# A two-layer encoder trunk: the input also laid out with features as rows, per-feature vectors as columns

## The chip, the core and the metric

The kernel runs on one core of a Trainium2 chip. The metric is the device time of one execution in microseconds, taken as the median of several runs; smaller is better. The engines are TensorE (PE in the profile; its weight loads are shown apart as PEld), VectorE (DVE), ScalarE (ACT), GpSimd (POOL) and SyncE (SP, which here only issues DMA loads and stores).

## The reference

The input `x` has 512 tokens of 1024 features, in float32. The first layer normalises each token (RMSNorm with a gain per feature, `a_norm_g`), multiplies by one wide input matrix, and splits the result into latents for attention, channels for pooling, and a gate. The second layer is a retention layer, and a last RMSNorm follows. The part that the change touches is the start of the first layer:

```python
def rms_norm(x, g):
    xf = x.astype(jnp.float32)
    y = xf * lax.rsqrt(jnp.mean(xf * xf, axis=-1, keepdims=True) + NORM_EPS)
    return (y * g.astype(jnp.float32)).astype(x.dtype)

def hybrid_attn_pool_layer(x, cos_a, sin_a, norm_g, w_in, ...):
    h = rms_norm(x, norm_g)
    proj = h @ w_in
    cq, ckv, kr, u, gate = jnp.split(proj, list(EVEN_SPLITS), axis=-1)
    ...
    y = jnp.concatenate([a, b], axis=-1) * jax.nn.silu(gate)
    return y @ w_out

x = x + hybrid_attn_pool_layer(x, ...)
```

`cq` (the query latents) are the first 384 columns of `proj`, `ckv` (the key and value latents) the next 128, `kr` the next 64. The per-feature vectors besides `a_norm_g` are the gains of the two latent norms, the scale of the pooling channels, the gain of the second layer's norm and the gain of its group norm: 3, 1, 8, 8 and 16 rows of 128.

## The kernel before

**Layout.** Features lie on the 128 partitions and the 512 tokens along the free dimension, so that `proj` comes out turned, 128 outputs by 512 tokens at a time. TensorE sums over the partitions, hence both the weights and the activations must have features on partitions. The weights lie so in memory; `x` lies with tokens as rows, and the kernel turns it on TensorE with an identity matrix (L264), 128 by 128 at a time, into PSUM.

**Precision.** Every product of two matrices is made of three (`mm3`, L71 to L76). Each operand is split into a high part, the value rounded to TensorE's fast float32 form, and a low part, what is left. ScalarE writes the high part (a copy, L108, L281), VectorE subtracts it for the low part (L109, L282). The products are high by high (L72), high weights by low activations (L75), and low weights by high activations (L76).

**The norm.** The gain per feature is applied before the product, as a scale per partition (L275 and L276, with the column `cols0`). The factor per token, called R, is applied behind it: squares of `x` by rows on ScalarE (L338, which adds up along the features), a sum (L340), the power of minus one half on GpSimd (L177), and a broadcast over all partitions on TensorE (`bcast`, L194 to L214: two products with a matrix of ones, L212 and L213), copied to SBUF by L343. `keep_R` (L332) multiplies a finished product by R while it empties the product's PSUM bank.

**The first stage.** `x_pair(q)` prepares two feature tiles: eight transpositions, the split of `x` times gain, the split of the weights of the 384 query latents, and a copy of the turned `x` to SBUF (L285, L286), which is later the residual. Four such pairs feed three outputs of 128 that are held in three PSUM banks (`held`), 72 products in all. Behind them comes the turn of the 36 per-feature rows into columns (L315), then R, then the 24 products of the key and value latents (`gemm_T`, L347), then 16 products for `kr` (L359, L360), then pooling and gates. Of PSUM's eight banks four have the name mm, two tr, two sc. With three held and one for the key and value latents, the bank for `kr` comes free when `keep_R` has run once.

**What sets the order.** The loads are issued by SP, in its program order, each landing at its own time; the weights go through four buffers (raw), split into four (wH) and three (wL). The first vector goes on ScalarE's queue. The framework's planner orders each engine's instructions beforehand: the earliest in program text that it reckons to be ready goes next. An instruction that is pinned (`keep_in_program_order`) is placed behind everything that was traced before it on its engine; what is traced after it may still be put ahead of it. The broadcast's first product (L212) and the instructions of `x_pair` on ScalarE and VectorE are pinned so. Six products with zeros (L160) run before the first load has landed.

Of the kernel before, what the change touches and what calls it, by code (L numbers as in the profile page):

```python
# [19 lines left out]
P = 128  # L20
# [12 lines left out]
QN, KVN, PSC, RN, GN = 0, 3, 4, 12, 20  # L33
NVEC = 36
# [3 lines left out]
def trunk(ctx: ExitStack, tc: tile.TileContext, x, positions, a_norm_g, a_w_in, a_q_norm_g, a_w_uq,  # L38
          a_kv_norm_g, a_w_ukv, a_pool_w, a_pool_scale, a_w_out, r_norm_g, r_w_in, r_decay_fwd,
          r_decay_bwd, r_gn_g, r_w_out, final_norm_g, freqs, edges, out):  # L40
# [9 lines left out]
    def S(tag, shape=(P, T), dt=F32):  # L50
        count[0] += 1
        return sb.tile(list(shape), dt, tag=tag, name=f"{tag}_{count[0]}", bufs=BUFS[tag])

    def C(name, shape, dt=F32):
        return sb.tile(list(shape), dt, tag=name, name=name, bufs=1)
# [61 lines left out]
    cols0 = C("cols0", (P, 8))  # L117
    cols = C("cols", (P, 40))[:, 0:NVEC]
# [11 lines left out]
    vrow0 = S("t")[:8, :P]  # L130
    nc.scalar.dma_start(vrow0, a_norm_g.rearrange("o (k p) -> (o k) p", p=P))

    pin(nc.scalar.copy(fsum[:, 0:4], mhalf))
    xt = [[None] * 4 for _ in range(4)]

    def load_x(q):
        for i in range(2):
            v = S("l1").rearrange("p (t n) -> p t n", t=2)
            nc.sync.dma_start(v, x[0, i * 256:(i + 1) * 256, q * 256:(q + 1) * 256]
                              .rearrange("(t p) n -> p t n", p=P))  # L140
            xt[2 * i][q] = v[:, 0]
            xt[2 * i + 1][q] = v[:, 1]
# [6 lines left out]
    def load_pair(q):  # L149
        load_x(q)  # L150
        raws.append(wload(w_in[q * 256:(q + 1) * 256, 0:384].rearrange("(k p) n -> p k n", p=P), 2, 384))
# [7 lines left out]
    for i in range(6):  # L159
        mm(warm, lhsT=zero[:, 0:P], rhs=zero, start=True, stop=True)  # L160
# [4 lines left out]
    vps = PS("tr")  # L165
    nc.tensor.transpose(vps[:, :8], vrow0, ident[:8, :8])
    pin(V.tensor_copy(cols0, vps[:, :8]))

# [87 lines left out]
    hH, hL, xT = [], [], []  # L256
    held = [PS("mm") for _ in range(3)]

    def x_pair(q):
        pts = []  # L260
        for k in (2 * q, 2 * q + 1):
            pt = PS(("tr", "tr", "sc", "sc")[k % 4])
            for t in range(4):
                i = nc.tensor.transpose(pt[:, t * P:(t + 1) * P], xt[t][q][:, (k % 2) * P:(k % 2 + 1) * P], ident)  # L264
                if q == 1:
                    pin(i)
            pts.append(pt)
        raw, n = raws[q][:2]
        wh = S("wH", (P, 1024), F32R)
        wl = S("wL", (P, 1024), F32R)  # L270
        for i in range(2):
            k = 2 * q + i
            h = S("hT", dt=F32R)
            l = S("hT", dt=F32R)
            pin(act(h, pts[i], AF.Copy, scale=cols0[:, k:k + 1]))  # L275
            pin(V.scalar_tensor_tensor(out=l, in0=pts[i], scalar=cols0[:, k:k + 1], in1=f(h), op0=ALU.mult,  # L276
                                       op1=ALU.subtract))
            hH.append(h)
            hL.append(l)
            c = slice(i * n // 2, (i + 1) * n // 2)  # L280
            pin(nc.scalar.copy(wh[:, c], raw[:, c]))  # L281
            pin(V.tensor_sub(wl[:, c], raw[:, c], f(wh[:, c])))  # L282
        u = [w[:, :n].rearrange("p (k n) -> p k n", k=2) for w in (wh, wl)]
        xT.extend([S("xT"), S("xT")])
        pin(nc.scalar.copy(xT[-2], pts[0]))  # L285
        pin(V.tensor_copy(xT[-1], pts[1]))  # L286
        return u
# [6 lines left out]
    nc.sync.dma_start(posi, positions[0].partition_broadcast(P))  # L294
    for q in range(4):
        if 0 < q < 3:
            us.append(x_pair(q + 1))
        uH, uL = us[q]
        for k in (2 * q, 2 * q + 1):
            if k == 1:  # L300
                us.append(x_pair(1))
            for m in range(3):
                ms = slice(m * P, (m + 1) * P)
                mm3(held[m], uH[:, k % 2, ms], uL[:, k % 2, ms], hH[k], hL[k], k == 0, k == 7)

    pin(V.tensor_copy(posf, posi))
    vrow = S("t")[:NVEC, :P]
    for src, at, n in ((a_q_norm_g, QN, 3), (a_kv_norm_g, KVN, 1),
                       (a_pool_scale, PSC, 8), (r_norm_g, RN, 8), (r_gn_g, GN, 16)):
        nc.sync.dma_start(vrow[at:at + n, :], src.rearrange("o (k p) -> (o k) p", p=P))  # L310
# [3 lines left out]
    vps = PS("tr")  # L314
    nc.tensor.transpose(vps[:, :NVEC], vrow, ident[:NVEC, :NVEC])  # L315
    V.tensor_copy(cols, vps[:, :NVEC])

    def gemm_T(w, c0, nm, evac, hH, hL):

        for m in range(nm):  # L320
            uH, uL = w_cols(w, c0 + m * P)
            pt = PS("mm")
            for k in range(8):
                mm3(pt, uH[:, k], uL[:, k], hH[k], hL[k], k == 0, k == 7)
            evac(m, pt)
            tick(2)
# [8 lines left out]
    for q in range(4):  # L335
        for t in range(4):
            junk = S("t")
            act(junk[:, 0:256], xt[t][q], AF.Square, accum_out=ssq[:, 4 * t + q:4 * t + q + 1])  # L338
    ss = S("sm", (P, 4))
    V.tensor_reduce(out=ss, in_=ssq.rearrange("p (t q) -> p t q", q=4), axis=AX.X, op=ALU.add)  # L340
# [6 lines left out]
    gemm_T(w_in, 384, 1, keep_R, hH, hL)  # L347
# [715 lines left out]
```

## Time and profile before

| what | value |
|---|---|
| median of 3 runs | 794.64 us (794.26 to 794.81) |
| the profiled execution's own time | 794.41 us |
| its span, first to last instruction | 792.6 us |
| TensorE busy | 781.1 us, 99% |
| VectorE busy | 579.0 us, 73% |
| ScalarE busy | 403.4 us, 51% |
| moved by DMA | 80.91 MB, 102 GB/s on average |

The profile's times are microseconds from the start of the span. In a timeline each row gives the start, the duration, the engine, the line of the kernel, the operation, what is written and read, and how many instructions were merged into the row; in brackets stands the idle time of the engine before it and what ended it. TensorE's products overlap, so the distance between two starts tells their pace and the duration does not. A row of waits gives the engine and what it did, what it waited for, the sum, the number of times and the longest. A row of a stretch of time gives the stretch, its length, the busy time of each engine with its count of instructions, the granted clock of TensorE, the share of DMA and GB/s.

### The profile page before, as it was taken

Reading aid. Unit: us, or ns where it says so; the run is one execution under the profiler, and the core shown is the slowest. Engines: PE = TensorE matmul, PEld = TensorE weight load, DVE = VectorE, ACT = ScalarE, POOL = GpSimd, SP = SyncE. Lnnn points to the kernel's source line nnn. Section 1 sums busy time; section 2 is a strip of 40 time slices with the busy share of each in tenths; the row PEclk is TensorE's granted clock in tenths of the full one; section 3 lists DMA queues with packets and bytes.
Section 4 is the critical chain, followed back from the end, with each engine's and each line's share of the span. In section 5 each row is a group of like instructions: output and inputs, shape, how many; then the busy total and the mean of one; then the engine's idle time right before and its main releaser. Section 6 shows DMA issues by size and latency. Waiting matters only on the chain. (4 is left out here: it accounts for less than half of the span.)

```text
span 792.6 us, 9592 instructions
## 1 busy us (share of the span) xinstructions
PE 781.1 (99%) x3546; PEld 642.0 (81%) x3546; DVE 579.0 (73%) x938; ACT 403.4 (51%) x670; POOL 38.6 (5%) x60
## 2 busy tenths in 40 slices
PE   9999999999999999999999999999999999999996
PEld 7888888888888888888877888888888888888885
DVE  4689986768748677899679747787377884767845
ACT  6645346666626744318654832358333583334832
POOL 0010000000000000100010100100101001010003
PEclk9999999999999999999999999999999999999999
DMA  8722233132123312353315822447324373244202
GB/s 254 226 62 83 70 82 87 39 80 91 54 72 88 103 38 69 87 152 107 107 37 133 227 56 80 111 111 210 74 79 110 103 203 84 71 122 102 85 27 108
DMA packets 87832, 80.91 MB, mean 102 GB/s; under 512 B 7868, under 2 KB 67304, under 8 KB 87784
## 3 DMA queue, kind: packets, MB, share of 16 engines
q1 hardware_dynamic: 82984, 71.11, 29.8%
q0 software_dynamic: 4352, 8.39, 7.0%
q10 hardware_dynamic: 448, 0.79, 0.3%
q8 instruction: 28, 0.46, 0.2%
q14 instruction: 20, 0.16, 0.1%
HBM read 76.87 MB, written 2.10 MB: 100 GB/s over the span
## 5 line engine op out<-in xcount | busy, mean ns | idle before, releaser
L72 PE MATMUL mm<-hT,wH 128*128 128x512 f32 x352 | 139.0, 395 | 0.3 <-ACT wH L281 0.3
L75 PE MATMUL mm<-hT,wH 128*128 128x512 f32 x352 | 137.8, 392 | 0.0
L76 PE MATMUL mm<-hT,wL 128*128 128x512 f32 x352 | 137.8, 392 | 0.0
L108 ACT CAST wH<-raw 128x1024 fp32r<-128x1024 f32 (+3 forms) x77 | 70.7, 923 | 114.4 <-PE mm L75 91.3
L109 DVE TENSOR_TENSOR wL<-raw,wH 128x1024 fp32r<-128x1024 f32 (+3 forms) x77 | 81.4, 1059 | 13.1 <-issue 4.7
L72 PEld LDWEIGHTS mm<-hT,wH 128*128 128x128 f32 x352 | 66.5, 189 | 14.0 <-ACT wH L281 0.7
L76 PEld LDWEIGHTS mm<-hT,wL 128*128 128x128 f32 x352 | 66.5, 189 | 14.0 <-DVE wL L282 0.2
L75 PEld LDWEIGHTS mm<-hT,wH 128*128 128x128 f32 x352 | 66.5, 189 | 13.6
L784 ACT CAST wH<-raw 128x1024 fp32r<-128x1024 f32 x32 | 33.7, 1054 | 50.2 <-PE mm L76 20.2
L785 DVE TENSOR_TENSOR wL<-raw,wH 128x1024 fp32r<-128x1024 f32 x32 | 38.9, 1220 | 10.4 <-issue 7.2
L784 ACT CAST wH<-tw 128x1024 fp32r<-128x1024 f32 x24 | 25.1, 1047 | 40.9 <-PE mm L76 26.3
L904 ACT ACTIVATE wH<-raw,cols 128x512 fp32r<-128x512 f32 x32 | 21.4, 717 | 43.8 <-issue 32.8
L925 DVE SCALAR_TENSOR_TENSOR xT<-mm,sm,xT 128x512 f32<-128x512 f32 (+1 forms) x33 | 24.1, 731 | 25.1 <-PE mm L76 25.0
L75 PE MATMUL mm<-y,wH 128*128 128x512 f32 x96 | 37.2, 389 | 0.0
L76 PE MATMUL mm<-y,wL 128*128 128x512 f32 x96 | 37.2, 389 | 0.0
L72 PE MATMUL mm<-y,wH 128*128 128x512 f32 x96 | 37.2, 390 | 0.0
L785 DVE TENSOR_TENSOR wL<-tw,wH 128x1024 fp32r<-128x1024 f32 x24 | 29.3, 1220 | 2.8 <-PE tr L794 1.0
L794 PE MATMUL mm<-wL,hT 128*128 128x512 f32 x80 | 31.1, 389 | 0.0
L795 PE MATMUL mm<-wH,hT 128*128 128x512 f32 x80 | 31.1, 389 | 0.0
L792 PE MATMUL mm<-wH,hT 128*128 128x512 f32 x80 | 31.0, 389 | 0.0
L885 DVE TENSOR_TENSOR l<-mm,l 128x512 f32<-128x512 f32 x16 | 11.1, 692 | 23.9 <-PE mm L76 23.9
L504 DVE TENSOR_TENSOR xT<-mm,xT 128x512 f32<-128x512 f32 x24 | 16.4, 688 | 15.0 <-PE mm L76 14.8
(361 smaller groups left out, 1903.6 us busy)
## 6 DMA issues: line engine op xcount, KB each, us to landing
raw<-in_r_w_in_dram SPq DMA_DIRECT2D x48, 512.0 KB, 3.7
raw<-in_a_w_in_dram SPq DMA_DIRECT2D x25, 512.0 KB, 4.0
raw<-in_a_w_out_dram SPq DMA_DIRECT2D x16, 512.0 KB, 3.9
raw<-in_r_w_out_dram SPq DMA_DIRECT2D x16, 512.0 KB, 5.5
tw<-in_r_w_in_dram SPq DMA_DIRECT2D x8, 512.0 KB, 3.8
tw<-in_r_w_in_dram POOLq DMA_DIRECT2D x8, 512.0 KB, 6.6
raw<-in_r_w_in_dram POOLq DMA_DIRECT2D x8, 512.0 KB, 6.0
l<-in_x_dram SPq DMA_DIRECT2D x8, 256.0 KB, 4.7
```

What stands on the lines that cost most here:

```text
L72: i = mm(pt, lhsT=lH, rhs=rH, start=st, stop=False)
L75: mm(pt, lhsT=lH, rhs=rL, start=False, stop=False)
L76: mm(pt, lhsT=lL, rhs=rH, start=False, stop=sp)
L108: then(nc.scalar.copy(h[:, c], raw[:, c]))
L109: then(V.tensor_sub(l[:, c], raw[:, c], f(h[:, c])))
L784: nc.scalar.copy(wh, ws[i])
L785: V.tensor_sub(wl, ws[i], f(wh))
L792: mm(o, lhsT=lh, rhs=wh[:, c], start=first and i == 0 and k2 == 0, stop=False, skip_group_check=True)
L794: mm(o, lhsT=lh, rhs=wl[:, c], start=False, stop=False, skip_group_check=True)
L795: mm(o, lhsT=ll, rhs=wh[:, c], start=False, stop=last and k2 == 1, skip_group_check=True)
L904: act(wh[:, c], raw[:, c], AF.Copy, scale=g)
L925: V.scalar_tensor_tensor(out=a, in0=pt[:, :T // n], scalar=rs[:, t:t + 1], in1=a, op0=ALU.mult, op1=ALU.add)
```

## The change

The host hands over two more inputs: `x_turned`, the input with features as rows (8 tiles of 128 features by 512 tokens), and `vectors`, all 44 rows of per-feature vectors, `a_norm_g` among them, as 44 columns. The turned input is loaded straight into the eight tiles of the residual, one load per feature tile, each followed by that tile's weights. All transpositions of `x` and of the vectors go, with the copies of the turned input out of PSUM. `x` by rows is still needed for the squares; it is now loaded behind everything that the first products need, in eight loads of 128 tokens by 512 features, and squared in eight instructions instead of sixteen. The weights of the key and value latents are loaded ahead of it (`kv_raw`). Each `x_pair` is traced one step ahead of the products that use the pair before it. Eight products with zeros run at the start instead of six.

```diff
-QN, KVN, PSC, RN, GN = 0, 3, 4, 12, 20
-NVEC = 36
+AN, QN, KVN, PSC, RN, GN = 0, 8, 11, 12, 20, 28
+NVEC = 44
...
-    cols0 = C("cols0", (P, 8))
-    cols = C("cols", (P, 40))[:, 0:NVEC]
+    cols = C("cols", (P, 48))[:, 0:NVEC]
...
-    vrow0 = S("t")[:8, :P]
-    nc.scalar.dma_start(vrow0, a_norm_g.rearrange("o (k p) -> (o k) p", p=P))
+    nc.scalar.dma_start(cols, vectors)
 
     pin(nc.scalar.copy(fsum[:, 0:4], mhalf))
-    xt = [[None] * 4 for _ in range(4)]
-
-    def load_x(q):
-        for i in range(2):
-            v = S("l1").rearrange("p (t n) -> p t n", t=2)
-            nc.sync.dma_start(v, x[0, i * 256:(i + 1) * 256, q * 256:(q + 1) * 256]
-                              .rearrange("(t p) n -> p t n", p=P))
-            xt[2 * i][q] = v[:, 0]
-            xt[2 * i + 1][q] = v[:, 1]
+    xT = [S("xT") for _ in range(8)]
+    xt = []
...
     def load_pair(q):
-        load_x(q)
-        raws.append(wload(w_in[q * 256:(q + 1) * 256, 0:384].rearrange("(k p) n -> p k n", p=P), 2, 384))
+
+        raw = S("raw", (P, 1024))
+        for i in range(2):
+            k = 2 * q + i
+            nc.sync.dma_start(xT[k], x_turned[k])
+            nc.sync.dma_start(raw[:, i * 384:(i + 1) * 384], w_in[k * P:(k + 1) * P, 0:384])
+        raws.append(raw)
...
-    for i in range(6):
+    for i in range(8):
         mm(warm, lhsT=zero[:, 0:P], rhs=zero, start=True, stop=True)
...
-    vps = PS("tr")
-    nc.tensor.transpose(vps[:, :8], vrow0, ident[:8, :8])
-    pin(V.tensor_copy(cols0, vps[:, :8]))
...
     def x_pair(q):
-        pts = []
-        for k in (2 * q, 2 * q + 1):
-            pt = PS(("tr", "tr", "sc", "sc")[k % 4])
-            for t in range(4):
-                i = nc.tensor.transpose(pt[:, t * P:(t + 1) * P], xt[t][q][:, (k % 2) * P:(k % 2 + 1) * P], ident)
-                if q == 1:
-                    pin(i)
-            pts.append(pt)
-        raw, n = raws[q][:2]
         wh = S("wH", (P, 1024), F32R)
         wl = S("wL", (P, 1024), F32R)
         for i in range(2):
             k = 2 * q + i
             h = S("hT", dt=F32R)
             l = S("hT", dt=F32R)
-            pin(act(h, pts[i], AF.Copy, scale=cols0[:, k:k + 1]))
-            pin(V.scalar_tensor_tensor(out=l, in0=pts[i], scalar=cols0[:, k:k + 1], in1=f(h), op0=ALU.mult,
+            pin(act(h, xT[k], AF.Copy, scale=col(AN + k)))
+            c = slice(i * 384, (i + 1) * 384)
+            pin(nc.scalar.copy(wh[:, c], raws[q][:, c]))
+            pin(V.scalar_tensor_tensor(out=l, in0=xT[k], scalar=col(AN + k), in1=f(h), op0=ALU.mult,
                                        op1=ALU.subtract))
+            pin(V.tensor_sub(wl[:, c], raws[q][:, c], f(wh[:, c])))
...
-            c = slice(i * n // 2, (i + 1) * n // 2)
-            pin(nc.scalar.copy(wh[:, c], raw[:, c]))
-            pin(V.tensor_sub(wl[:, c], raw[:, c], f(wh[:, c])))
-        u = [w[:, :n].rearrange("p (k n) -> p k n", k=2) for w in (wh, wl)]
-        xT.extend([S("xT"), S("xT")])
-        pin(nc.scalar.copy(xT[-2], pts[0]))
-        pin(V.tensor_copy(xT[-1], pts[1]))
-        return u
+        return [w[:, :768].rearrange("p (k n) -> p k n", k=2) for w in (wh, wl)]
...
     nc.sync.dma_start(posi, positions[0].partition_broadcast(P))
+    kv_raw = wload(w_in[:, 384:512].rearrange("(k p) n -> p k n", p=P), 8, P)
+
+    for i in range(8):
+        v = S("l1")
+        nc.sync.dma_start(v, x[0, i // 2 * P:(i // 2 + 1) * P, i % 2 * T:(i % 2 + 1) * T])
+        xt.append(v)
     for q in range(4):
-        if 0 < q < 3:
+        if q < 3:
             us.append(x_pair(q + 1))
         uH, uL = us[q]
         for k in (2 * q, 2 * q + 1):
-            if k == 1:
-                us.append(x_pair(1))
...
-    vrow = S("t")[:NVEC, :P]
-    for src, at, n in ((a_q_norm_g, QN, 3), (a_kv_norm_g, KVN, 1),
-                       (a_pool_scale, PSC, 8), (r_norm_g, RN, 8), (r_gn_g, GN, 16)):
-        nc.sync.dma_start(vrow[at:at + n, :], src.rearrange("o (k p) -> (o k) p", p=P))
...
-    vps = PS("tr")
-    nc.tensor.transpose(vps[:, :NVEC], vrow, ident[:NVEC, :NVEC])
-    V.tensor_copy(cols, vps[:, :NVEC])
-
-    def gemm_T(w, c0, nm, evac, hH, hL):
+    def gemm_T(w, c0, nm, evac, hH, hL, first=None):
 
         for m in range(nm):
-            uH, uL = w_cols(w, c0 + m * P)
+            uH, uL = wsplit(*first) if first else w_cols(w, c0 + m * P)
...
-    for q in range(4):
-        for t in range(4):
-            junk = S("t")
-            act(junk[:, 0:256], xt[t][q], AF.Square, accum_out=ssq[:, 4 * t + q:4 * t + q + 1])
+    for i in range(8):
+        act(S("t"), xt[i], AF.Square, accum_out=ssq[:, i:i + 1])
     ss = S("sm", (P, 4))
-    V.tensor_reduce(out=ss, in_=ssq.rearrange("p (t q) -> p t q", q=4), axis=AX.X, op=ALU.add)
+    V.tensor_reduce(out=ss, in_=ssq[:, 0:8].rearrange("p (t q) -> p t q", q=2), axis=AX.X, op=ALU.add)
...
-    gemm_T(w_in, 384, 1, keep_R, hH, hL)
+    gemm_T(w_in, 384, 1, keep_R, hH, hL, kv_raw)
...
+    given['x_turned'] = np.ascontiguousarray(given['x'][0].T).reshape(8, P, T)
+    given['vectors'] = np.ascontiguousarray(np.concatenate(
+        [given[n].reshape(-1, P) for n in ('a_norm_g', 'a_q_norm_g', 'a_kv_norm_g', 'a_pool_scale', 'r_norm_g',
+                                           'r_gn_g')]).T)
```

More of the change, by code (lines that the diff above doesn't have):

```diff
@@ L39, in trunk @@
           a_kv_norm_g, a_w_ukv, a_pool_w, a_pool_scale, a_w_out, r_norm_g, r_w_in, r_decay_fwd,
-          r_decay_bwd, r_gn_g, r_w_out, final_norm_g, freqs, edges, out):
+          r_decay_bwd, r_gn_g, r_w_out, final_norm_g, freqs, edges, x_turned, vectors, out):
     nc = tc.nc
@@ L253, in tables @@
         return c, s
-    hH, hL, xT = [], [], []
+    hH, hL = [], []
     held = [PS("mm") for _ in range(3)]
     def x_pair(q):
-        pts = []
-        for k in (2 * q, 2 * q + 1):
-            pt = PS(("tr", "tr", "sc", "sc")[k % 4])
-            for t in range(4):
-                i = nc.tensor.transpose(pt[:, t * P:(t + 1) * P], xt[t][q][:, (k % 2) * P:(k % 2 + 1) * P], ident)
-                if q == 1:
-                    pin(i)
-            pts.append(pt)
-        raw, n = raws[q][:2]
         wh = S("wH", (P, 1024), F32R)
```

## The prediction

> **What bounds the kernel now.** I read the busy times first, then what TensorE (PE) waited for over the whole span, then the timeline of the first 38 us, since the diff touches nothing later.
>
> ```profile
> PE 781.1 (99%) x3546; PEld 642.0 (81%) x3546; DVE 579.0 (73%) x938; ACT 403.4 (51%) x670; POOL 38.6 (5%) x60
> ```
>
> ```profile
> PE sc L160 <- POOL t L157: 1.3, 1, 1.3
> PE sc L72 <- ACT qk L81: 1.2, 1, 1.2
> PE tr L792 <- DVE t L826: 0.7, 1, 0.7
> PE mm L794 <- DVE wL L785: 0.6, 1, 0.6
> PE mm L792 <- DVE t L835: 0.5, 1, 0.5
> PE mm L72 <- ACT wH L281: 0.3, 1, 0.3
> ```
>
> The six waits are all that TensorE has: 4.6 us of 792.6. After its first real product it runs back to back, so whatever leaves its stream before the tail comes off the end, as long as its operands keep coming. Now the stream itself:
>
> ```profile
> 1.33 2.93 PE L160 MATMUL sc<-t 128*128 128x512 f32 x6 [1.33 <-POOL t L157]
> 4.39 2.23 PE L264 MATMUL tr<-ident,l 128*128 128x128 f32 x8
> 5.08 1.14 PEld L264 LDWEIGHTS tr<-ident,l 128*128 128x128 f32 x6 [0.40 <-DMA l<-in_x_dram]
> 5.81 0.69 ACT L275 ACTIVATE hT<-tr,cols 128x512 fp32r<-128x512 f32 x1 [2.94 <-PE tr L264]
> 6.40 0.50 ACT L281 CAST wH<-raw 128x384 fp32r<-128x384 f32 x1
> 6.95 0.80 PE L72 MATMUL mm<-hT,wH 128*128 128x512 f32 x1 [0.32 <-ACT wH L281]
> ...
> 10.53 0.39 PE L76 MATMUL mm<-hT,wL 128*128 128x512 f32 x1
> 10.76 1.04 PE L264 MATMUL sc<-ident,l 128*128 128x128 f32 x8
> 11.55 0.48 PE L72 MATMUL mm<-hT,wH 128*128 128x512 f32 x1
> ...
> 27.52 0.39 PE L76 MATMUL mm<-hT,wL 128*128 128x512 f32 x1
> 27.84 0.25 PE L315 MATMUL tr<-ident,t 36*128 36x36 f32 x1
> 28.02 0.50 PE L212 MATMUL tr<-t,ones 128*128 128x512 f32 x1
> 28.35 0.39 PE L213 MATMUL tr<-t,ones 128*128 128x512 f32 x1
> 28.58 0.39 PE L72 MATMUL mm<-hT,wH 128*128 128x512 f32 x1
> ...
> 34.05 0.39 PE L359 MATMUL mm<-hT,wH 128*128 128x512 f32 x1
> ```
>
> Starts count here, since durations overlap. The held stage is 72 products (8 feature tiles, 3 outputs, 3 products), the first at 6.95, the last at 27.52. At full pace one follows another by 0.23 (24 from 28.58 to 34.05 are 5.47, so 0.228 each). The first nine take 3.81 (6.95 to 10.76), not 2.05: 1.76 lost to a half-speed start, though the clock column of the windows below says 1.00 there. The other 63 are 14.36, and 16.76 pass from 10.76 to 27.52: with 62 paces of 14.14 to the last start, 2.62 is left for three groups of eight transpositions, 0.87 a group. Together: 71 paces (16.19) + 1.76 + 2.62 = 20.57, which is 27.52 - 6.95.
>
> **Part 1: transpositions leave: 2.62 + 0.2.** Three groups stand between products and cost 2.62. The fourth is ahead of the first product (part 2). The turn of the 36 per-feature rows (L315) makes 27.52 to 28.02 cost 0.50 where one pace would do: 0.2 to 0.27, I take 0.2. All of it lies on TensorE's full stream.
>
> The Trainium skill prices a transposition at about 275 ns in a kernel (TensorE: Matmul & The Clock Gate, Part 4: PE-mode transpose). This trace has 0.11 of stream per transposition (0.87 for eight), so the trace decides; by the page 24 would be worth an estimated 6.6 us and the sum 4.0 more.
>
> **Part 2: the first product comes earlier: 1.75.** Now it needs two x loads, a w load for two feature tiles, eight transpositions at half speed, then 1.14 on ScalarE (5.81 to 6.95). After, it needs one 262 kB load of x turned, one 197 kB load of w, the vectors (23 kB, on ScalarE's queue, as the 4 kB were), and the same 1.14.
>
> ```profile
> 1.80:6.00 4.20, 4.20 (x14) 2.74 (x14) 0.17 (x1) 1.25 (x3) 0.20 (x3) 1.00 0.94 286
> 1.80:13.50 11.70, 11.37 (x41) 8.26 (x41) 4.50 (x9) 6.94 (x18) 0.20 (x3) 1.00 1.01 337
> 9.00:13.50 4.50, 4.50 (x23) 3.71 (x22) 1.87 (x4) 2.69 (x9) 0.00 (x0) 1.00 1.07 384
> ```
>
> The last number is GB/s. At 286 from 1.8 on, the second x load (0.52 MB in all) is moved by 3.6 and was waited for until 5.08: landing comes up to 1.4 behind the bytes. The first x load had landed by 4.39. So the turned x lands between 2.7 and 4.39, its w (0.46 MB in all) between 3.4 and 5.08. ScalarE then starts by 4.4, casts by about 4.7, and the first product comes at 4.9 to 5.6; I take 5.2, gain 1.75. The eight zero products fill TensorE: the six end at 4.26, so the next could start at about 4.1 (0.43 each but the first), and two more last to 4.9, just ahead of it, so they cost 0 (cover: the wait for w; were w to land at 3.4, 0.3). The low halves come from VectorE 0.6 later, which stretches the first three products: -0.15. Bounds of the part: 1.2 to 1.9.
>
> **Part 3: the slow start: 1.06 (0 to 1.76).** Full pace came 3.6 us after the first real product, and six zero products (2.7 us) had not brought it. Eight zero products are 3.6 us. If any unbroken run of products of that length brings it, all 1.76 is won; if only real products count, 1.6 is lost again (8 paces by 0.2) and 0.16 won. I take 0.7 still lost.
>
> The Trainium skill (the same page, Part 1: The HAM clock gate) says that a busy window of about 3.4 us releases the gate, that the window runs freely and that the release varies by run. The single release seen here, 3.6 after 6.95, agrees with the length and can't show the phase; by the page the loss lies anywhere in these bounds.
>
> **Part 4: copies leave, operands from SBUF: 0.** Four ScalarE copies of 0.59 (L285) and four VectorE copies of 0.68 (L286) go. Per feature tile ScalarE has 0.69 + 0.51 left and VectorE 0.75 + 0.55, below TensorE's 9 x 0.228 = 2.05. A scaled copy from SBUF takes 0.713 where one from PSUM takes 0.69 (first the groups by line, with busy us and mean ns; then three lines by themselves, with least, median and most ns):
>
> ```profile
> L276 DVE SCALAR_TENSOR_TENSOR hT<-tr,cols,hT 128x512 fp32r<-128x512 f32 x4 | 3.0, 748 | 1.9 <-ACT hT L275 1.9
> L281 ACT CAST wH<-raw 128x384 fp32r<-128x384 f32 x8 | 4.0, 506 | 0.0
> L282 DVE TENSOR_TENSOR wL<-raw,wH 128x384 fp32r<-128x384 f32 x8 | 4.4, 548 | 0.0
> L338 ACT ACTIVATE t<-l 128x256 f32<-128x256 f32 x16 | 6.5, 421 | 0.0
> ```
>
> ```profile
> L904 ACT ACTIVATE wH<-raw,cols x32: 706/713/727, 468.7 to 751.8; 128x512 fp32r<-128x512 f32 x32
> L285 ACT COPY xT<-tr x2: 593/596/599, 7.8 to 16.3; 128x512 f32<-128x512 f32 x2
> L286 DVE COPY xT<-tr x2: 683/685/687, 8.8 to 17.3; 128x512 f32<-128x512 f32 x2
> ```
>
> It is worth 0 because neither engine ends last here; without that cover 0.02 per tile would be lost, 0.2. Five small loads leave SP's queue.
>
> **Part 5: x by rows moves behind everything: 0 (0 to -3).** Only the sums of squares need it now, and they make R.
>
> ```profile
> 24.10 0.20 ACT L338 ACTIVATION_READ_ACCUMULATOR t<-l 128x1 f32 x1
> 24.33 0.17 DVE L340 TENSOR_REDUCE sm<-ssq 128x4 f32<-128x16 f32 x1 [1.00 <-ACT t L338]
> 26.37 1.28 ACT L210 ACTIVATE t<-ident,sm 128x128 fp32r<-128x128 f32 x4 [1.13 <-DVE sm L203]
> 29.96 0.57 ACT L343 COPY R<-tr 128x512 f32<-128x512 f32 x1
> 31.52 1.88 DVE L332 TENSOR_TENSOR y<-mm,R 128x512 f32<-128x512 f32 x3
> ```
>
> On SP stand 16 loads (3.67 MB), positions (0.26), the latent weights (0.52, waiting for the first raw buffer, which VectorE frees after the first pair, 2.6 after 4.9 and so at 7.5, while the 18 loads ahead of it on SP are still being issued; queued behind that wait is x by rows) and x by rows (2.10): 6.55 MB. 3.94 MB are moved by 13.5 (337 GB/s), the rest at 384 by 20.3; it lands, with half the lag seen, at 21.0. One more square of 512 (twice 0.42 at most) to 21.8, then the chain from 24.30 to 27.65 above, 3.35: the broadcast (L212) can start at 25.2. Now it could at 27.65 and started at 28.02.
>
> TensorE ends the 72 at about 22.5 (5.2 + 0.15 + 72 x 0.228 + 0.7). Next to do are 24 products of the latent weights, which are in by then and take the fourth mm bank, until 28.0. If the planner lets them pass L212, nothing waits; R is copied at about 26.5 and the first bank emptied by 27.3. That it does so shows here:
>
> ```profile
> 37.67 0.39 PE L72 MATMUL mm<-hT,wH 128*128 128x512 f32 x1
> ...
> 52.18 0.39 PE L184 MATMUL tr<-t,ones 128*128 128x512 f32 x1
> ```
>
> L184 is pinned behind the 48 products of pool_in(0), yet 64 paces lie between 37.67 and 52.18: 16 products traced after it went ahead.
>
> **Sum.** 2.62 + 0.2 + 1.75 - 0.15 + 1.06 + 0 + 0 = 5.5 us. The profiled execution took 794.41 (span 792.6 and 1.8 around it): 788.9. The median is 0.23 above it, so **789.1** for the median.
>
> **Rivals.**
> The zero products don't count. Then part 3 is 0.16: gain 4.6, 790.0. For: six didn't help. Against: they made 2.7 us, short of 3.6.
>
> The planner puts L212 straight behind the 72. TensorE then stands from 22.5 to 25.2; the 24 and L213 follow, L359 at 25.2 + 0.23 + 0.33 + 5.47 = 31.2, 2.8 before 34.05: 791.8. For: today L212 stands there. Against: the passing above.
>
> VectorE becomes the bound.
>
> ```profile
> 60.00:100.00 40.00, 40.00 (x176) 32.68 (x175) 38.72 (x65) 17.67 (x26) 0.00 (x0) 1.00 0.24 71
> ```
>
> It is busy 38.72 of 40 there. If its work hangs on R and R comes only 2.8 earlier (25.2 for 28.02), TensorE can't run further ahead: 791.8 again. Against: TensorE never waits for it there.
>
> **Slower: the loads lose pace.** x is read twice, and w in halves. Mechanism: R late while all four mm banks wait for it, so that L359 stands. From L212 to a free bank are about 2.0 (0.6 of products, 0.57 for the copy of R, 0.63 for the first of three L332, 0.2 of hand-overs). L359 is as late as now when L212 comes at 32.05, so the last x at 27.1 moved: 6.55 MB in 25.3 us, 258 GB/s. Below that it is slower; at 230, 3.1 later: 797.5. Against: 337 GB/s with loads of 262 and 393 kB, several under way. The Trainium skill asks for 1 MiB per DMA (DMA: Bandwidth & Descriptors, Bandwidth) and gives 138 GB/s at 64 KB, 341 at 1 MB; taken alone a load of 262 kB would by its fit come to an estimated 101 GB/s, the slower side. No run here shows loads one at a time.
>
> **Chances.** Forecast 0.50, zero products don't count 0.17, L212 first 0.15, VectorE 0.10, loads 0.05, something else 0.03. A measurement of this kernel can't tell less than 0.2% (1.6 us) from none. The first four gain 2.8 and more: faster 0.92, with 0.05 for same (a stall longer than reckoned) and 0.03 slower. The range goes from all of part 3 won and the first product at 4.9 (gain 2.62 + 0.2 + 1.9 + 1.76 = 6.5, so 788.2; to 787.4 for 0.8 of the 4.6 of waits that a new plan may lose) up to the two 2.8 cases and 0.6 more, 792.4.
>
> **What would show it.** First product at 4.9 to 5.6. Products 0.23 apart from there (part 3 won) or 0.43 until about 8.6 (zero products don't count). No 128x128 transposition before the scores. 72nd product at 21.3 to 23. L212 amid the latent products, with no PE idle before it (a wait of PE for ACT or DVE there is the second rival). L359 at about 28.5. The forecast is wrong if L359 is 5 earlier and the end is not, or if the last x lands after 23.

## The result and the profile after

The changed kernel takes 789.17 us (median, 788.71 to 789.68), beside 794.45 (792.79 to 795.43) for the kernel before on the same chip: ratio 0.9936, 95% interval 0.9923 to 0.9949. A second set of runs gave 789.34 beside 793.27, 0.9946 (0.9930 to 0.9963). The forecast was 789.1. The profiled execution took 788.88 (span 787.1); before it was 794.41 (792.6).

In the changed kernel the lines have moved: zero products L156, pairs of operands L258 to L263 (L275 to L282 before), squares L311 (L338), broadcast of R L204 and L205 (L212, L213), copy of R L316 (L343), the four y = product x R L307 (L332), products of kr L332 and L333 (L359). First the busy times of the changed kernel, then two of the five waits that its TensorE has (us in total, times, longest):

```profile
PE 775.6 (99%) x3514; PEld 637.3 (81%) x3514; DVE 576.2 (73%) x932; ACT 400.6 (51%) x650; POOL 38.6 (5%) x60
```

```profile
PE sc L72 <- ACT qk L81: 1.2, 1, 1.2
PE mm L332 <- DVE y L307: 0.7, 1, 0.7
...
```

TensorE is busy 5.5 us less, which is the gain, and still 99% of the span. One wait is new: kr for VectorE's y (L307). The wait ahead of the first product and the 0.5 of mm for t are gone in this execution. The stages, from the timeline (start, length, engine, line, ...):

```profile
1.34 3.78 PE L156 MATMUL sc<-t 128*128 128x512 f32 x8 [1.34 <-POOL t L153]
4.92 0.90 PE L72 MATMUL mm<-hT,wH 128*128 128x512 f32 x2
5.65 0.61 PE L75 MATMUL mm<-hT,wH 128*128 128x512 f32 x2
5.98 0.73 ACT L258 ACTIVATE hT<-xT,cols 128x512 fp32r<-128x512 f32 x1 [1.15 <-DMA xT<-in_x_turned_dram]
7.24 0.42 PE L72 MATMUL mm<-hT,wH 128*128 128x512 f32 x1
8.35 0.40 PE L72 MATMUL mm<-hT,wH 128*128 128x512 f32 x1
...
21.75 0.39 PE L76 MATMUL mm<-hT,wL 128*128 128x512 f32 x1
21.92 0.61 ACT L311 ACTIVATE t<-l 128x512 f32<-128x512 f32 x1
24.69 1.28 ACT L202 ACTIVATE t<-ident,sm 128x128 fp32r<-128x128 f32 x4 [2.06 <-DVE sm L195]
26.51 0.39 PE L204 MATMUL tr<-t,ones 128*128 128x512 f32 x1
26.96 0.39 PE L205 MATMUL tr<-t,ones 128*128 128x512 f32 x1
27.39 0.59 ACT L316 COPY R<-tr 128x512 f32<-128x512 f32 x1 [0.91 <-PE tr L205]
27.64 0.39 PE L76 MATMUL mm<-hT,wL 128*128 128x512 f32 x1
28.00 2.48 DVE L307 TENSOR_TENSOR y<-mm,R 128x512 f32<-128x512 f32 x4 [0.80 <-ACT R L316]
28.75 0.50 PE L332 MATMUL mm<-hT,wH 128*128 128x512 f32 x1 [0.72 <-DVE y L307]
```

No 128x128 transposition stands in the stretch. The first product comes at 4.92, 2.03 earlier than before. A step is the distance from one product's start to the next. The first step takes 0.50 (the second product starts at 5.42), the others 0.227 (5.65 to 7.24 are seven steps, the doubled rows counted), except where the second tile's operands are late (7.24 to 8.35 is 1.11 for three). The 72nd product of the held stage starts at 21.75 (before: 27.52). L204 stands amid the latent products with no wait ahead of it: 20 of the 24 have passed it. Then, between the last latent product at 27.64 and kr at 28.75, TensorE stands; VectorE's first y, which frees an mm bank, begins only at 28.00.

| stage, profiled executions | before | after | won so far |
|---|---|---|---|
| first product | 6.95 | 4.92 | 2.03 |
| 72nd product | 27.52 | 21.75 | 5.77 |
| kr (L359, now L332) | 34.05 | 28.75 | 5.30 |
| the execution's own time | 794.41 | 788.88 | 5.53 |

### The profile page after: what moved, and what is told of

It is laid out like the page before. It is cut to its first block, busy times and chain, and to the rows that moved or that the text cites. A ratio compares the mean times of both kernels' runs of the same rounds, so it can differ in the third digit from the quotient of the medians.

```text
span 787.1 us, 9514 instructions
## 1 busy us (share of the span) xinstructions
PE 775.6 (99%) x3514; PEld 637.3 (81%) x3514; DVE 576.2 (73%) x932; ACT 400.6 (51%) x650; POOL 38.6 (5%) x60
## 4 chain that ended last, share of the span: by engine, by line
PE 84%; issue 10%; DVE 3%; POOL 1%; ACT 0%; POOLq 0%; DVEq 0%
PE mm L72 19%; PE mm L76 19%; PE mm L75 19%; PE mm L767 4%; PE mm L768 4%; PE mm L765 4%; PE tr L548 2%; PE sc L72 2%; PE sc L76 2%; PE sc L75 2%; PE sc L767 1%; PE sc L768 1%; PE sc L765 1%; PE sc L529 1%; PE sc L530 1%
## 5 line engine op out<-in xcount | busy, mean ns | idle before, releaser
L72 PE MATMUL mm<-hT,wH 128*128 128x512 f32 x352 | 138.0, 393 | 0.0
L72 PEld LDWEIGHTS mm<-hT,wH 128*128 128x128 f32 x352 | 66.2, 188 | 13.8 <-ACT wH L260 0.7
L72 PE MATMUL mm<-y,wH 128*128 128x512 f32 x96 | 37.2, 390 | 0.0
```

The costliest lines, as they stand in the source:

```text
L72: i = mm(pt, lhsT=lH, rhs=rH, start=st, stop=False)
```

## Experiments

Times are medians; where kernels of different chips stand side by side, their ratios to the kernel before on the same chip decide.

**The transpositions put back.** 24 transpositions of tiles already there, pinned in the places of the old ones, with results that nothing reads:

```diff
         for k in (2 * q, 2 * q + 1):
+            if k in (1, 2, 4):
+                for g in range(2):
+                    idle = PS("tr")
+                    for t in range(4):
+                        pin(nc.tensor.transpose(idle[:, t * P:(t + 1) * P], xT[k - g][:, t * P:(t + 1) * P], ident))
```

> The changed kernel with 24 idle 128x128 transpositions of the turned input put back at the three places where they stood between products; nothing reads them. By the row of before (0.87 for eight) the 72nd product comes 2.6 later, at 24.3; as this covers the 0.88 wait for R, the first kr product comes 1.7 later, at 30.5, and the time is 1.7 us longer. By 275 ns for one, the page's price, the 72nd comes 6.6 later and the time is 5.7 us longer.

Measured: 791.16, ratio 0.9961 (0.9947 to 0.9976). TensorE's timeline of this kernel:

```profile
10.38 0.39 PE L72 MATMUL mm<-hT,wH 128*128 128x512 f32 x1
10.62 1.91 PE L289 MATMUL tr<-ident,xT 128*128 128x128 f32 x16
...
12.59 0.40 PE L76 MATMUL mm<-hT,wL 128*128 128x512 f32 x1
...
16.00 0.40 PE L76 MATMUL mm<-hT,wL 128*128 128x512 f32 x1
16.23 1.04 PE L289 MATMUL tr<-ident,xT 128*128 128x128 f32 x8
...
17.34 0.39 PE L75 MATMUL mm<-hT,wH 128*128 128x512 f32 x1
```

From the product ahead of the sixteen to the second product behind them pass 2.21, where two steps would be 0.45; for the eight it is 1.34 (the step from the first product behind a group to the second is long too, 0.31). That is 1.76 and 0.89, 2.65 in all and 0.11 each; the trace of before gave 2.62.

The time can't be read off so simply. In this execution full pace came later too (at 7.3), and the 72nd product starts at 25.09, 3.34 after that of the changed kernel. kr comes at 31.21, 2.46 later, since it doesn't wait here: the planner put the broadcast behind 79 products, where in the changed kernel it stands behind 92, and so R is there in time. The profiled time is 2.41 longer. By the medians the loss is 1.2 to 2.0 (0.9961 less 0.9946 or 0.9936, of the 793.36 of the kernel before); 1.7 was expected. The sum with the Trainium skill's 275 ns a transposition (TensorE: Matmul & The Clock Gate, Part 4: PE-mode transpose) is refuted: 24 of them take 2.65 us of stream here and not 6.6.

**The zero products: none, six, and eight before the change.** In the changed kernel the loop of eight is taken out, or made six; in the kernel before six are made eight; and the kernel before is profiled once more as it is.

```diff
-    warm = PS("sc")
-    for i in range(8):
-        mm(warm, lhsT=zero[:, 0:P], rhs=zero, start=True, stop=True)
```

> The changed kernel without any zero product. Theory A (an unbroken run of products of about 3.5 us brings full pace, and zero products count): first real product at 4.9 as now, starts 0.43 apart until about 8.5 and 0.23 after; the 72nd product starts at about 23.0 where it is at 21.7 now (1.76 lost, 0.4 of it won back from the wait for the second tile). R hangs on the loads and comes no later, so the 0.88 wait for the first kr product is covered: that product comes 0.2 to 0.5 later than 28.75, and the whole is 0.3 to 0.5 us longer. Theory B (zero products don't count, full pace came by luck of the run): pace and time as in the changed kernel.

> The changed kernel with six zero products as before the change: they end at 4.1, then TensorE idles 0.8 to the first real product. Theory A in its strict form (the run must be unbroken): slow until about 8.5, as without any. Theory A in its loose form (work is added up over a window): full pace somewhere between 4.9 and 8.5. Theory B: as in the changed kernel. Time at most 0.5 us above the changed kernel in every case, since R covers it.

> The kernel before with eight zero products instead of six, nothing else. They last to 4.9, about as long as the second load of x takes to land (5.08). Theory A: the transpositions behind them and the first real products run at full pace, the first kr product comes at about 32 instead of 34.05, time 2 us (1.8 to 2.3) less than before. Theory B: it comes at 34.0 to 34.5, time the same or up to 0.5 us more.

> The kernel before, unchanged, for a second profile of its start. Theory A' (the window of the clock gate runs freely, so the moment of full pace is a matter of the run): full pace comes at another time than 3.6 after the first real product, anywhere from before it to 10.5. If the run of products decides: again 3.6 after it, at 10.5.

Measured: without zero products 789.69, ratio 0.9940 (0.9921 to 0.9960); with six 789.98, 0.9948 (0.9931 to 0.9964), in single times of 789.09, 789.09 and 789.48 and again of 790.47, 790.97 and 791.19; the kernel before with eight 793.36, ratio 1.0000 (0.9988 to 1.0012); the kernel before again 793.13 in its one execution. TensorE's timelines, of the changed kernel without zero products and then of the kernel before in its second profile:

```profile
4.89 0.79 PE L72 MATMUL mm<-hT,wH 128*128 128x512 f32 x1 [4.89 <-ACT wH L257]
...
9.25 0.40 PE L75 MATMUL mm<-hT,wH 128*128 128x512 f32 x1
...
29.27 0.39 PE L329 MATMUL mm<-hT,wH 128*128 128x512 f32 x1
```

```profile
6.91 0.50 PE L72 MATMUL mm<-hT,wH 128*128 128x512 f32 x1 [0.41 <-ACT wH L281]
...
8.10 0.39 PE L72 MATMUL mm<-hT,wH 128*128 128x512 f32 x1
8.33 0.40 PE L75 MATMUL mm<-hT,wH 128*128 128x512 f32 x1
...
26.76 0.50 PE L212 MATMUL tr<-t,ones 128*128 128x512 f32 x1
```

Three things follow. The slow start of before was one execution's: in this other one a product lasts 0.50 from the first on and not 0.80, three steps lose 0.51 (6.91 to 8.10, for operands) and then 0.23 is the pace, and the broadcast (L212) comes at 26.76 and not at 28.02. In the kernel before, two more zero products win nothing in the median; its profile has full pace at the first real product, which comes 0.4 later there (7.35). And the eight zero products of the changed kernel seem to be worth nothing in the time, though without them the first ten steps take 4.36 (4.89 to 9.25), 2.09 over full pace: kr comes only 0.52 later (29.27 for 28.75), and no longer waits. The planner's order is another one as well: the broadcast stands behind 84 products, not behind 92. That made the wait the next suspect.

With six, the profile (of the execution of 789.09) has full pace at the first real product, though TensorE had idled 0.61 just ahead of it. So six zero products were enough in that execution, and the gap behind them did no harm. What splits the six times into two groups, no profile here shows.

**kr on another bank, with and without the zero products.** kr's products write a bank of the score pool; the order of work on the engines stays. The changed kernel itself ran beside it.

```diff
-    krp = PS("mm")
+    krp = PS("sc")
```

> Edit: in the changed kernel the products of kr (L332, L333) write a bank of the score pool instead of one of the four mm banks. Theory (the 0.88 us for which TensorE stands ahead of kr at 27.87 is for the mm bank that the first of the four keep_R on VectorE frees): kr needs none of them, comes at about 27.9 right behind the last latent product, and the time falls by the wait, 0.7 to 0.9 us, to about 788.3 where the changed kernel has 789.2. Rival A (what ends last is the split of kr's weights on VectorE, which now stands just ahead of keep_R): kr still comes at 28.7 and the time stays. Rival B (the wait moves to the next mm bank, the first product of the scores' operands behind kr): kr comes 0.9 earlier, a wait of about the same length follows it, and the time stays.

> The changed kernel without any edit, as the reference beside the other three. Theory (full pace comes within a window that each execution begins anew somewhere, and the eight zero products count for it): first product at 4.9 again, full pace from somewhere between 4.9 and 7.4, kr at 28.5 to 29.3, 788.7 to 789.7 us. Rival (full pace at about 5.4 is fixed by the eight zero products): the same start to 0.2 us as in its first profile.

> The edit of kr_sc, and the eight zero products left out. Without them and with kr on an mm bank, kr came only 0.52 later though 10 products had gone at half pace (2.0 lost): the wait ahead of kr covered most of it. Theory (the wait for the bank was the cover): with the wait gone the start costs its whole length, kr comes 1.3 to 2.0 later than in kr_sc, and the time is 1.2 to 1.8 above kr_sc. Rival (the cover was chance, full pace came at another moment in that execution): within 0.6 of kr_sc.

Measured, all on one chip: 788.06 (787.98 to 788.87, ratio 0.9934, 0.9919 to 0.9948), beside 789.34 (788.77 to 789.68, 0.9946) for the changed kernel and 789.94 (789.39 to 790.42, 0.9954, 0.9938 to 0.9971) without zero products. The timelines of TensorE and VectorE, of kr on the score bank and then of the same without zero products:

```profile
27.70 0.39 PE L76 MATMUL mm<-hT,wL 128*128 128x512 f32 x1
27.93 0.39 PE L332 MATMUL sc<-hT,wH 128*128 128x512 f32 x1
28.07 2.48 DVE L307 TENSOR_TENSOR y<-mm,R 128x512 f32<-128x512 f32 x4 [0.47 <-ACT R L316]
...
31.55 0.39 PE L72 MATMUL mm<-hT,wH 128*128 128x512 f32 x1
```

```profile
4.93 0.80 PE L72 MATMUL mm<-hT,wH 128*128 128x512 f32 x1 [4.93 <-ACT wH L257]
...
11.00 0.40 PE L76 MATMUL mm<-hT,wL 128*128 128x512 f32 x1
...
30.05 0.39 PE L329 MATMUL sc<-hT,wH 128*128 128x512 f32 x1
```

The wait was for the bank: kr follows the last latent product by 0.23, before VectorE has begun its first y (28.07), 0.86 earlier than in the changed kernel's second profile (28.79), and no wait follows. The time falls by 1.28, somewhat over the 0.7 to 0.9 expected; the sixteen steps from kr to the next L72 also take 3.62 and not 3.80, so that the next L72 comes 1.04 earlier (31.55 for 32.59). This version is the fastest of all here: its five times and the five of the changed kernel overlap by 0.1.

Why the bank is free so late shows in the changed kernel's second profile:

```profile
21.62 0.62 ACT L311 ACTIVATE t<-l 128x512 f32<-128x512 f32 x1
24.39 1.28 ACT L202 ACTIVATE t<-ident,sm 128x128 fp32r<-128x128 f32 x4 [2.06 <-DVE sm L195]
26.55 0.39 PE L204 MATMUL tr<-t,ones 128*128 128x512 f32 x1
```

The last square begins 0.30 earlier than in the first profile, and the broadcast's operands are all ready by about 25.7 (24.39 + 1.28; in the first profile by about 26.0); yet the broadcast comes 0.04 later, and kr waits as long. In both it stands where the planner put it, behind 92 of the 96 products of the held stage and the latents. From its start 2.24 us pass until kr has a bank. The broadcast's two products and the last four of the latents fill 1.36 of them; for the other 0.88 TensorE stands. Where the planner put it earlier (84 products ahead of it without zero products, 79 with the transpositions back), kr doesn't wait, though it writes an mm bank there too.

Without zero products and without that wait, the first fourteen steps take 6.07 where full pace would be 3.18 (4.93 to 11.00); kr comes 2.12 later (30.05) and the median is 1.88 higher, just past the 1.2 to 1.8 expected; in the profiled executions it is 2.40. So the zero products are worth 1.9 when nothing behind them waits. In the changed kernel the wait for the bank, which the kernel without zero products doesn't have, hid that.

Full pace came in the profiles with eight zero products at different moments: at 4.1 with kr on the score bank (two zero products start 0.31 apart), at 5.4 and 5.5 in the two of the changed kernel, at 6.7 with the positions moved (below), at 7.3 with the transpositions put back; without them 4.0 us after the first product in one execution and 5.7 in the other. Products with zeros count: full pace was there before a real product had run. That the two profiles of the changed kernel agree to 0.2 is what the rival said, that eight fix the moment; 4.1 and 7.3 with the same eight zero products ahead, begun at the same 1.33, speak against it. The Trainium skill (TensorE: Matmul & The Clock Gate, Part 1: The HAM clock gate) says that the activity window runs freely, and these profiles agree.

**The positions' load moved behind x by rows.** The row of positions, which is written to all 128 partitions (262 kB in all), stood ahead of the latent weights and x by rows on SP. Here it is issued behind them, and its cast on VectorE stands behind the copy of R.

```diff
     posi = S("V", dt=I32)
-    nc.sync.dma_start(posi, positions[0].partition_broadcast(P))
     kv_raw = wload(w_in[:, 384:512].rearrange("(k p) n -> p k n", p=P), 8, P)
...
         xt.append(v)
+    nc.sync.dma_start(posi, positions[0].partition_broadcast(P))
...
-    pin(V.tensor_copy(posf, posi))
...
     nc.scalar.copy(R, rp)
+    pin(V.tensor_copy(posf, posi))
```

> The changed kernel with the load of the positions moved behind the loads of x by rows, and the conversion of the positions traced behind the copy of R; nothing else. Theory A (the 0.88 wait of the first kr product is R, and R hangs on the loads ahead of it): x by rows lands 1.5 earlier, at 20.2, the broadcast's first product starts at about 25.1 instead of 26.5, the first kr product follows the latent products without a wait at 27.9 instead of 28.75, and the time is 0.9 us less. Rival (the wait comes from the place that the planner gives the broadcast, not from the loads): it goes only if the broadcast moves in the order too, and then with unchanged landing.

Measured: 792.44 (790.76 to 793.28), ratio 0.9977 (0.9967 to 0.9986): slower than the changed kernel by 2.5 to 3.3. From the timeline of this kernel:

```profile
25.88 0.39 PE L204 MATMUL tr<-t,ones 128*128 128x512 f32 x1
27.47 0.62 ACT L328 CAST wH<-raw 128x512 fp32r<-128x512 f32 x1
27.61 2.48 DVE L306 TENSOR_TENSOR y<-mm,R 128x512 f32<-128x512 f32 x4 [2.78 <-ACT R L315]
30.01 0.68 DVE L329 TENSOR_TENSOR wH<-raw,wH 128x512 fp32r<-128x512 f32 x1
30.75 0.77 PE L332 MATMUL mm<-hT,wH 128*128 128x512 f32 x1 [2.44 <-DVE wH L329]
...
34.27 0.40 PE L332 MATMUL mm<-hT,wH 128*128 128x512 f32 x1
```

The last x by rows lands at 20.88 and not 21.72, the broadcast comes 0.63 earlier and the first y 0.39. The broadcast owes that to its place and not to the loads: its operands are ready by about 25.0, and its two products come in their turn at 25.88 and 26.56, now behind 88 products. So the rival has the cause of the wait. But the planner now also put the split of kr's weights on ScalarE (L328) behind the copy of R, and so its second half on VectorE (L329) behind all four y, 2.5 us; in the changed kernel they stood ahead, at 25.88 and 26.51. kr waits 2.44 for them, and after that wait eight steps take 3.52 (30.75 to 34.27) instead of 1.82. The gain was lost to a new order of the work.

**x by rows loaded twice.** 2.10 MB more on SP ahead of the x that the squares read, first with a small copy of each dummy load on VectorE, then with no reader at all.

```diff
+    for i in range(8):
+        nc.sync.dma_start(S("qk"), x[0, i // 2 * P:(i // 2 + 1) * P, i % 2 * T:(i % 2 + 1) * T])
     for i in range(8):
         v = S("l1")
```

> The changed kernel with x by rows loaded a second time, into tiles of which one column each is copied and nothing is used, ahead of the loads that the squares need: 2.1 MB more before R. The mechanism of the slower rival (R late while all four mm banks wait): R comes 5.2 later (eight loads of 0.64), its broadcast at about 31.2, the first kr product at 33.9 instead of 28.75, about where it was before the change; time 5.2 us more than the changed kernel, within 1 us of the kernel before. If the planner finds other products to fill the wait, less than 2 us more.

> The changed kernel, with the 2.10 MB of x by rows loaded once more into buffers that nothing reads, ahead of the x by rows that the squares read. Nothing else waits for the second copy. Theory (R's way to the first free mm bank sets kr, and x by rows sets R): last x by rows lands 5.2 to 5.5 later, at about 27; the broadcast follows at about 31.5, kr at about 33.5 to 34 after TensorE has stood for some 5 us; the time rises by 5, to about 794.2, and by 1.6 to 1.8 more, to about 796, if half pace follows the long wait as it did behind the wait of 2.6 with the positions last. Rival (other work of VectorE and the planner's slack take the delay up): below 792.

Measured: 802.59 (ratio 1.0112, 1.0096 to 1.0128) with the small copies. That run doesn't test what it was made for: the copies hung on the dummy loads and stood ahead of the pinned pairs on VectorE, and TensorE stood for 12.34 us amid the held stage. Without readers 796.89 (795.85 to 797.44), ratio 1.0038 (1.0021 to 1.0054). Of this one the timeline, and one stretch by itself (us, busy of PE, PEld, DVE, ACT and POOL, granted clock, DMA share, GB/s):

```profile
28.42 0.61 ACT L313 ACTIVATE t<-l 128x512 f32<-128x512 f32 x1
32.01 0.77 PE L204 MATMUL tr<-t,ones 128*128 128x512 f32 x1 [4.68 <-DVE lg L625]
33.97 2.48 DVE L309 TENSOR_TENSOR y<-mm,R 128x512 f32<-128x512 f32 x4 [0.27 <-ACT R L318]
34.72 0.79 PE L334 MATMUL mm<-hT,wH 128*128 128x512 f32 x1 [1.40 <-DVE y L309]
```

```profile
34.70:38.30 3.60, 3.58 (x9) 2.81 (x10) 3.60 (x5) 2.07 (x3) 0.00 (x0) 0.50 0.95 286
```

Here the planner put the broadcast behind all 96 products, and it waits for its operands (the row names the VectorE instruction that stands behind the one that writes them). This is the chain of the prediction, taken to where it decides: the last square starts 6.50 later than in the changed kernel (the 5.2 to 5.5 expected of the load was short by 1.0), the broadcast 5.50, kr 5.93 (34.72 for 28.79), and the profiled time is 796.89, 7.69 above 789.20. The rest, 1.76, is half pace: the eight steps from 34.72 on take 3.58 (0.59 and seven of 0.43) instead of 1.82. The row grants 0.50 of the clock there. L204 stands at 32.01, almost at the 32.05 from which the slower rival reckons a loss; that rival left out the half pace.

**Loads cut in two.** Every load of x turned, of its weights and of x by rows is issued as two halves (131 and 98 kB): the slower rival by itself.

```diff
-            nc.sync.dma_start(xT[k], x_turned[k])
-            nc.sync.dma_start(raw[:, i * 384:(i + 1) * 384], w_in[k * P:(k + 1) * P, 0:384])
+            for c in range(2):
+                nc.sync.dma_start(xT[k][:, c * 256:(c + 1) * 256], x_turned[k][:, c * 256:(c + 1) * 256])
...
+                nc.sync.dma_start(raw[:, i * 384 + c * 192:i * 384 + (c + 1) * 192],
...
-        nc.sync.dma_start(v, x[0, i // 2 * P:(i // 2 + 1) * P, i % 2 * T:(i % 2 + 1) * T])
+        for c in range(2):
+            nc.sync.dma_start(v[:, c * 256:(c + 1) * 256],
```

> The changed kernel with every load of x turned, of its weights and of x by rows cut in two (131 and 98 kB each). If the rate falls with the size of a load, as the slower rival has it, x by rows lands later than 21.7 and the end moves with it: at 0.33 to 0.43 for an issue on SP, 51 loads take about 20 us to issue, so I expect landing at 23 to 25, the first kr product at 30.1 to 32 and 1.4 to 3.2 us more. If the rate hangs only on the bytes, everything is as in the changed kernel.

Measured: 800.78 (800.27 to 801.27), ratio 1.0087 (1.0073 to 1.0101): 11 to 12 above the changed kernel, where 1.4 to 3.2 were expected. A stretch of the loads in this kernel, then its timeline:

```profile
1.80:13.50 11.70, 11.24 (x42) 8.32 (x42) 5.95 (x10) 6.79 (x12) 0.20 (x3) 1.00 0.82 234
```

```profile
27.05 0.43 SPq L295 DMA_DIRECT2D edge<-in_edges_dram  x1
27.53 0.43 SPq L296 DMA_DIRECT2D dec<-in_r_decay_fwd_dram  x1
33.23 0.47 PE L207 MATMUL tr<-t,ones 128*128 128x512 f32 x1 [1.20 <-DVE lg L628]
38.03 0.79 PE L337 MATMUL mm<-hT,wH 128*128 128x512 f32 x1 [3.79 <-DVE wH L334]
```

At 234 GB/s (some 240 up to the last x, which lands at 29.55), under the rival's 258, the kernel is slower than before, as that rival said. Its price was too small: by its rule kr would come 1.2 after its old 34.05 (33.23 for 32.05), and it came at 38.03, because the split of kr's weights fell behind the four y here too (3.79 of wait), and half pace follows. What sets this pace is in the SP rows: a load is issued in 0.43 and the next begins 0.48 after it, whatever its size, so a mean 115 kB gives about 240, and the DMA engines are busy for 0.82 of the stretch. The changed kernel's loads of 262 and 197 kB make 334 and then 389 (below), at a share of 1.00 and 1.06. The Trainium skill (DMA: Bandwidth & Descriptors, Bandwidth) asks for loads of 1 MiB, from figures of loads that GpSimd issues: that small loads cost pace is borne out here by 234 beside 334 in the same stretch, but loads of 262 and 197 kB, several under way, already made 334.

## Why the prediction was right, and where its steps were not

The time is within 0.1 of the forecast (789.17 for 789.1), and the chain is the one that was named: work leaves a TensorE that is hardly ever idle, and the end follows. That it came so close is luck in part, as the points show. For the profiled execution:

- **Part 1**, 2.62 + 0.2: right. No transposition is left, and putting 24 back costs 2.65 of stream. From the 72nd product through the two broadcasts, three steps of 0.23 stand where 0.50, 0.33 and 0.23 stood: 0.37, not 0.2.
- **Part 2**, 1.75 less 0.15 for a stretch (1.2 to 1.9 in all): 2.03 less 0.43, so the 1.60 came out, by two errors that cancel. The loads land as early as the better bound allowed. The stretch was mis-sized: it was reckoned for VectorE's low halves, and what was late was the second turned x, for which ScalarE waited 1.15 (L258 at 5.98). That the earlier first product is worth its 2.03 is read from the timeline; no experiment tests it by itself.
- **Part 3**, 1.06: 1.49 in this execution, where only the first step is slow, by 0.27. The step that failed is the reasoning, not the sum. It took the slow start as the kernel's own, and it is an execution's: before loses 1.76 in one profile and 0.51 in the other, and eight zero products in the kernel before changed nothing in its median. The medians of the two sets differ by 5.3 and 3.9; how much of that difference is this, no run here shows. What the zero products do by themselves is seen only with the bank's wait gone: 1.9.
- **Part 4**, 0: right. TensorE waits for no copy; the pairs are 0.726 and 0.496 on ScalarE (L258, L260), 0.752 and 0.552 on VectorE.
- **Part 5**, 0 (0 to -3): -0.88, a term missed. The forecast had R copied at 26.5 and the first bank free by 27.3, just ahead of the last latent product. R was copied at 27.39, and the bank came free at about 28.6 (28.00 and a quarter of 2.48). The broadcast, forecast for 25.2, came in its turn among the latent products, at 26.51 and 26.96. The last square was late too, by 0.8 (it began at 21.92, where it was to end at 21.8), but that didn't decide: L202 was done at about 26.0 (24.69 + 1.28), 1.0 ahead of the second product's turn, and the second profile has the operands at 25.7 and the same wait. That the planner lets the latent products pass L204, taken from the old L184, was right; that this passing itself delays R was not reckoned.
- The sum: 5.77 at the 72nd product (5.28 reckoned), 5.30 at kr (5.5), 5.53 at the end. So the sum is right partly by errors that cancel: +0.28 for the first product, -0.28 for the stretch, +0.43 for the slow start, +0.17 behind the 72nd, -0.88 at kr, and +0.23 behind kr. And 1.49 of it hang on how these two executions began: the other profile of before loses 1.25 less at its start.

The rivals. "Zero products don't count" falls: full pace came while only zero products had run. "L204 straight behind the 72" didn't happen. "VectorE becomes the bound" neither. The row that spoke for it has grown a little, yet TensorE has no wait there. The stretches of the changed kernel, the loads first:

```profile
1.80:13.50 11.70, 11.70 (x43) 8.76 (x43) 7.98 (x14) 9.21 (x17) 0.20 (x3) 1.00 1.00 334
18.00:21.00 3.00, 3.00 (x15) 2.49 (x14) 0.97 (x1) 3.00 (x11) 0.00 (x0) 1.00 1.06 389
60.00:100.00 40.00, 40.00 (x176) 32.83 (x176) 38.94 (x64) 15.09 (x20) 0.00 (x0) 1.00 0.27 78
```

The slower rival's place, R late behind slow loads, is confirmed by the halves. Its threshold of 258 is only bracketed, by 234 and 334, and its price was too small; the loads here keep 334 and 389. Not tried was a kernel in which VectorE's load between 60 and 100 us is changed, so how near that bound is stays open.

## What to carry to other kernels

On an engine that never waits, a removed instruction is worth its start-to-start distance in the stream, and that can be summed from the trace to a few tenths of a us. After such a cut look at once for the first place where the stream now catches up with something slower: here a PSUM bank was waited for, 0.9 us, since the broadcast that frees it stood too near the end of the products ahead, and giving one group a bank of another pool won it back. A gain found at the head of a kernel is hidden by any wait behind it, so test it with that wait removed; and a slow start seen in one profile needs a second profile before it is priced.

## What the runs showed that was not expected

- **A wait of 2.4 us brought half pace back, waits of 1.2 or less did not.** After kr's wait of 2.44 (positions moved) 1.70 are lost, after the 4.68 and 1.4 of x twice 1.76. In the halves two waits close together did it, 1.71 and 0.53: from 25.32 seven steps take 3.11 and not 1.59. After the 0.7 ahead of kr, and the 1.2 further on, the pace stays. The Trainium skill (TensorE: Matmul & The Clock Gate, HAM oscillation) puts the limit at gaps over about 3.4 us; here 2.44 was enough.
- **The clock column is blind at the start.** It shows 0.50 for the half pace behind the wait of x twice, but 1.00 for the same pace at the start of before. There the starts have to be read.
- **Full pace comes at another moment in each execution**, 4.1 to 7.3 with the same eight zero products, and the two profiles of the kernel before differ by 1.3 at L212 for it.
- **Issue of loads, not bytes, can set the pace**: 0.48 from one load to the next on SP, and 234 GB/s at 131 and 98 kB.
- **The planner's order is a cost of its own.** With one load moved, the broadcast came 0.6 earlier and the kernel was some 3 us slower, as one split changed its place on VectorE.
